# Twenty matmuls on a constant tile, and a later place for the second token half, ahead of and in the first SwiGLU of an encoder trunk

## The chip, the cores and the metric

The kernel runs on one core of a Trainium2 chip. The metric is device time in microseconds of one execution. TensorE does the matrix products (PE in the profile; PEld is its loading of weights), VectorE (DVE) and ScalarE (ACT) the elementwise work, GpSimd (POOL) a little of the setup, SyncE (SP) issues the transfers. Each engine takes its own instructions in the order in which they are queued, and waits where an instruction needs something that isn't there yet.

## What is computed

Two groups of tokens (512 and 256, width 1024) go through two layers with shared weights. Each layer is half a SwiGLU, a mixer, half a SwiGLU, each with an RMSNorm ahead and a residual; a last RMSNorm follows.

```
def swiglu(h, wg, wu, wd):
    return (jax.nn.silu(h @ wg) * (h @ wu)) @ wd

def even_layer(x, f1_n, f1_g, f1_u, f1_d, mix_n, ...):
    x = x + 0.5 * swiglu(rmsnorm(x, f1_n), f1_g, f1_u, f1_d)
...
```

The change concerns the first of the four SwiGLUs: `wg` and `wu` are 1024 x 2816, `wd` is 2816 x 1024, all float32.

## The kernel before

All activations lie transposed: `x[m]`, m = 0 to 7, is a tile of 128 features by 768 tokens. The tokens are treated as two halves of 384 (`HALVES`, h = 0 and 1). Products are made of float32 operands split in a rounded high part and a remainder: `mm3` issues three matmuls (high by high, high by low, low by high). For a weight, the high part is a cast on ACT (`whi`, line 111) and the remainder a subtraction on DVE (`wlo`, line 112); five buffers of each exist.

The gate and up products of the SwiGLU are done by a Strassen-like scheme with seven products in place of eight: the features are cut in m < 4 and m >= 4, the tokens in the two halves, the output columns in pairs of 128-wide tiles ("pairs", `NPAIR` = 11). The right-hand operands are called b11, b21 (first token half, m < 4 and m >= 4), t2, t3, t1, n4, b22 (combinations that need the second half). The left-hand ones are weights or sums of weights (`sums`, line 580). One product for gate or up is 4 x 3 = 12 matmuls with 384 moving columns, so a step for gate and up is 24.

The combinations are prepared from x by `feed` (line 312). For h = 0, `gain_split` makes b11 or b21 directly. For h = 1 and m < 4 it subtracts the first half on DVE (line 327); for m >= 4 it scales by the norm's gain on ACT (line 329); when both features of an index are there, `combine` (DVE, line 348) and `split` (ACT line 193, DVE line 194) make t2. `rest` (line 350) then makes t3, t1, n4 and b22. The norm itself is applied later: `norm_add` squares x on ACT (lines 213, 216) and adds the squares on DVE (line 217); `norm_tok` sums over the features on PE against a tile of ones and takes the inverse root by 13 small DVE steps (lines 258 to 269); `norm_spread` puts the result on a diagonal (lines 247, 249) and spreads it on PE by `onesr`; line 388 copies it to where `hidden` (lines 481 to 484) multiplies by it.

The order on PE is the order in which the program issues; the other engines are ordered by a scheduler at build time. Work that runs beside the products is written as generators, which `tick` advances behind each `mm3` by a clock of the planner, `self.t`: a matmul of n columns adds n/2400 us, at least 0.107, and a float32 one four times that. `norm_half` waits on that clock `DELAY0` = (7, 11) us for the first half and `DELAY1` = (26, 12) for the second ahead of the sums and ahead of the spread. `run_until` sets the clock forward where the program needs a result that isn't issued yet.

The first three pairs (`EARLY`) begin ahead of the rest, in steps that `ORDER` = (0, 1, 0, 1, 0, 2, 1, 2, 2) gives: pair 0's products on b11, pair 1's on b11, pair 0's on b21, pair 1's on b21, pair 0's `hidden(0, 0)`, and so on. A product on b11 is copied from its bank on ACT (tile p, line 497), because b21's products are added into the same bank while the other products need p1 alone. These copies are collected in `copied`: the first two are those of pair 0 (gate, up), the next two those of pair 1. Behind these steps, pair 0 is done in the order p6 (t2), p7 (t3), p5 (t1), p3 (b22), p4 (n4), with `hidden(1, 1)` behind p5, the first that needs the second half's norm.

For the first SwiGLU, the work on the second token half is issued by `second` (line 371). `issue_after(ins)` keeps the instructions of its block that run on the same engine as `ins` (here ACT) behind `ins` in that engine's queue; instructions of the block on other engines get no such bound. In the kernel before, both passes of the loop (first `feed`, then `norm_add`) wait until two copies have been issued by the program, and are queued behind `copied[1]`.

Of the kernel before, what the change touches and what calls it, by code (L numbers as in the profile page):

```python
# [16 lines left out]
P = 128  # L17
# [21 lines left out]
NMASK = 8 * (24 + 32 + 24) + 4 * (40 + 40)  # L39
NE = 30  # L40
EARLY = 3
ORDER = (0, 1, 0, 1, 0, 2, 1, 2, 2)

WTOTAL = 12 * D * FF + 8 * EARLY * P * D + D * 1792 + 2 * D * D + D * 3072 + D * 512
GAP0 = 4.6
# [4 lines left out]
class Trunk:  # L50
# [320 lines left out]
    def second(self):  # L371

        for n in (1, 2):
            while len(self.copied) < 2:
                yield 0.2
            with self.tc.issue_after(self.copied[1]):
                for m in [i // 2 + (0 if i % 2 else 4) for i in range(KD)]:
                    if n == 1:
                        self.feed(m, 1)
                    else:  # L380
                        self.norm_add(m, H, T)
        self.half_done(1)
# [8 lines left out]
    def ffn(self, pre):  # L391
# [42 lines left out]
        def pair(p):  # L434

            early = p < EARLY
            names = ("gate", "up")
# [117 lines left out]
        stages = [pair(p) for p in range(NPAIR)]  # L555
        for p in ORDER:
            next(stages[p])
# [826 lines left out]
    def build(self):  # L1384
        nc = self.nc
        self.ident = self.cp.tile([P, P], F32, tag="ident", name="ident")
        make_identity(nc, self.ident)
        self.ones = self.cp.tile([P, P], F32, tag="ones", name="ones")
        nc.gpsimd.memset(self.ones, 1.0)
        self.onesr = self.cp.tile([P, P], F32R, tag="onesr", name="onesr")  # L1390
        nc.vector.tensor_copy(self.onesr, self.ones)
        self.gains = self.cp.tile([P, KD * len(NORMS)], F32, tag="gains", name="gains")
        nc.scalar.dma_start(self.gains, self.aps["gains"])
        self.ngains = self.cp.tile([P, KD * len(NORMS)], F32, tag="ngains", name="ngains")
        nc.gpsimd.tensor_scalar(out=self.ngains, in0=self.gains, scalar1=-1.0, scalar2=None, op0=ALU.mult)
        self.x = [self.xp.tile([P, T], F32, tag=f"x{m}", name=f"x{m}") for m in range(KD)]
        todo = [KIND[p] for p in self.phases] + [("last", 6)]
        kind = todo[0][0]
        if kind == "f":
            self.ffn_open("right")  # L1400
            self.ffn_tiles()
            self.fw = self.open("work", "left")
        elif kind != "last":
            self.mixer_tiles("right")
        self.norm_begin(todo[0])
        for h, (c0, c1) in enumerate(HALVES):
            for m in range(KD):
                nc.sync.dma_start(self.x[m][:, c0:c1], self.aps["x"][m, :, c0:c1])
                if not (h and kind == "f"):
                    self.final(m, c0, c1)  # L1410
                if h == 0 and m % 4 == 3 and kind == "f":
                    pre = f"{self.phases[0][:2]}_ffn{self.phases[0][3]}"
                    self.first += [self.raw(f"{pre}_w_{n}", 0, KD, m // 4 * 2 * P, P) for n in ("gate", "up")]
            if h and kind == "f":
                self.spawn(self.second())
            elif kind in ("f", "last"):
                self.half_done(h)
            if kind == "last":
                self.drain()
        for i, ph in enumerate(self.phases):  # L1420
            self.following = todo[i + 1]
            if i == 0 and "l1m" in self.phases:
                self.bias_tables()
            if ph == "l1m":
                while self.spare:
                    self.spare.pop(0)()
            if ph == "l0m":
                self.mixer0()
            elif ph == "l1m":
                self.mixer1()  # L1430
            else:
                self.ffn(f"{ph[:2]}_ffn{ph[3]}")
        self.drain()
        for n in list(self.guards)[::-1]:
            self.close(n)
# [103 lines left out]
```

## Time and profile before

| | |
|---|---|
| device time, median of 3 runs | 2689.56 us (2686.41 to 2692.57) |
| profiled execution, span from first to last instruction | 2689.7 us |
| PE busy | 2594.1 us (96%) |
| DVE busy | 2309.7 us (86%) |
| ACT busy | 1399.3 us (52%) |
| first product of the first SwiGLU | at 8.42 us |
| mean granted TensorE clock | 0.981 |

The page gives no time of the profiled execution but its span, so that span stands for it; it is 0.1 us above the median of the runs. In rows of a timeline the columns are start, duration, engine, line, operation, output<-inputs, shapes, and in brackets the idle time ahead with what ended it. Busy rows overlap a little, since an instruction may start before the one ahead of it has drained: what an instruction costs in a full queue is the distance between starts.

### The profile page before, as it was taken

Reading aid. Unit: us, or ns where it says so; the run is one execution under the profiler, and the core shown is the slowest. Engines: PE = TensorE matmul, PEld = TensorE weight load, DVE = VectorE, ACT = ScalarE, POOL = GpSimd, SP = SyncE. Lnnn points to the kernel's source line nnn. Section 1 sums busy time; section 2 is a strip of 40 time slices with the busy share of each in tenths; the row PEclk is TensorE's granted clock in tenths of the full one; section 3 lists DMA queues with packets and bytes.
Section 4 is the critical chain, followed back from the end, with each engine's and each line's share of the span. In section 5 each row is a group of like instructions: output and inputs, shape, how many; then the busy total and the mean of one; then the engine's idle time right before and its main releaser. Section 6 shows DMA issues by size and latency. Waiting matters only on the chain.

```text
span 2689.7 us, 41021 instructions
## 1 busy us (share of the span) xinstructions
PE 2594.1 (96%) x14950; PEld 2530.4 (94%) x14950; DVE 2309.7 (86%) x4865; ACT 1399.3 (52%) x2915; POOL 91.0 (3%) x172
## 2 busy tenths in 40 slices
PE   7999999999999999999999999999999989999997
PEld 6999999977889999999999999988888989999997
DVE  8988888789769988898998888877777699888886
ACT  6545444555655544455654454455555465454443
POOL 0000000000100000000000000012121100000000
PEclk9999999999999999999999999989999999999999
DMA  5332222321222222222322222231211322222121
GB/s 168 111 94 89 79 63 88 132 71 44 79 75 95 73 69 79 66 76 79 95 79 73 69 76 70 83 116 50 62 60 37 95 87 86 79 63 79 63 87 55
DMA packets 82745, 214.78 MB, mean 80 GB/s; under 512 B 19952, under 2 KB 32752, under 8 KB 82544
## 3 DMA queue, kind: packets, MB, share of 16 engines
q1 hardware_dynamic: 82400, 212.14, 24.7%
q8 instruction: 117, 1.92, 0.3%
q14 instruction: 84, 0.69, 0.1%
q10 hardware_dynamic: 144, 0.03, 0.0%
HBM read 202.70 MB, written 15.07 MB: 81 GB/s over the span
## 4 chain that ended last, share of the span: by engine, by line
PE 88%; DVE 8%; ACT 2%; issue 1%; DMA 0%; SPq 0%; DVEq 0%; ACTq 0%
PE ps_mm L137 56%; PE ps_aux L137 31%; DVE wlo L112 1%; PE ps_aux L141 1%; DVE kl L1140 1%; DVE xl L710 1%; ACT whi L111 0%; DMA raw<-in_w 0%; DVE tl L194 0%; DVE qk L1327 0%; DVE kl L1142 0%; ACT xh L709 0%; DVE p L893 0%; DVE p L878 0%; DVE x L677 0%
## 5 line engine op out<-in xcount | busy, mean ns | idle before, releaser
L111 ACT CAST whi<-s 128x512 fp32r<-128x512 f32 x496 | 302.1, 620 | 378.0 <-DVE s L580 142.7
L111 ACT CAST whi<-raw 128x512 fp32r<-128x512 f32 x512 | 309.9, 619 | 260.9 <-PE ps_mm L137 127.2
L112 DVE TENSOR_TENSOR wlo<-s,whi 128x512 fp32r<-128x512 f32 x496 | 335.5, 685 | 74.7 <-ACT whi L111 74.3
L112 DVE TENSOR_TENSOR wlo<-raw,whi 128x512 fp32r<-128x512 f32 x494 | 336.9, 690 | 23.5 <-ACT whi L111 20.4
L137 PE MATMUL ps_aux<-dt,whi 128*128 128x384 f32 x864 | 221.6, 338 | 0.0
L137 PE MATMUL ps_mm<-db,whi 128*128 128x384 f32 x864 | 221.6, 338 | 0.0
L137 PEld LDWEIGHTS ps_mm<-db,whi 128*128 128x128 f32 x864 | 156.8, 188 | 0.0
L137 PEld LDWEIGHTS ps_aux<-dt,whi 128*128 128x128 f32 x864 | 156.8, 188 | 0.0
L137 PE MATMUL ps_mm<-xh,whi 128*128 128x512 f32 (+1 forms) x416 | 148.3, 357 | 2.9 <-ACT xh L709 2.9
L137 PE MATMUL ps_mm<-xl,whi 128*128 128x512 f32 (+1 forms) x416 | 145.0, 348 | 1.1 <-DVE xl L710 1.1
L137 PE MATMUL ps_mm<-db,wlo 128*128 128x384 f32 x432 | 146.0, 338 | 0.0
L137 PE MATMUL ps_aux<-dt,wlo 128*128 128x384 f32 x432 | 145.9, 338 | 0.0
L137 PE MATMUL ps_mm<-xh,wlo 128*128 128x512 f32 (+1 forms) x416 | 144.5, 347 | 0.0
L580 DVE TENSOR_TENSOR s<-raw,raw 128x512 f32<-128x512 f32 x124 | 83.4, 685 | 21.6 <-DMA raw<-in_w 21.4
L467 ACT COPY u<-ps_mm 128x384 f32<-128x384 f32 x176 | 83.6, 475 | 35.0 <-PE ps_mm L137 34.9
L472 DVE TENSOR_TENSOR u<-ps_aux,u 128x384 f32<-128x384 f32 x176 | 97.1, 551 | 5.0 <-PE ps_aux L137 3.8
L137 PE MATMUL ps_aux<-dh,whi 128*128 128x384 f32 x384 | 98.5, 338 | 0.7 <-DVE x L677 0.7
L884 ACT ACTIVATE p<-p,st 128x192 f32<-128x192 f32 (+2 forms) x144 | 68.8, 480 | 54.9 <-DVE st L882 54.9
L632 DVE TENSOR_TENSOR x<-ps_aux,x 128x384 f32<-128x384 f32 x160 | 86.6, 552 | 11.2 <-PE ps_aux L137 11.0
L580 DVE TENSOR_TENSOR s<-raw 128x512 f32<-128x512 f32 x124 | 84.9, 685 | 11.8 <-DMA raw<-in_w 11.3
L137 PE MATMUL ps_mm<-oh,whi 128*128 128x384 f32 x256 | 89.4, 349 | 4.0 <-DVE x L861 4.0
L632 DVE TENSOR_TENSOR x<-ps_mm,x 128x384 f32<-128x384 f32 x160 | 87.0, 551 | 6.0 <-PE ps_mm L137 5.9
(438 smaller groups left out, 8204.5 us busy)
## 6 DMA issues: line engine op xcount, KB each, us to landing
raw<-in_w SPq DMA_DIRECT2D x342, 512.0 KB, 3.6
xdm<-x SPq DMA_DIRECT2D x16, 384.0 KB, 2.4
x<-in_x SPq DMA_DIRECT2D x16, 192.0 KB, 5.7
x<-xdm SPq DMA_DIRECT2D x8, 384.0 KB, 3.8
xold<-xdm SPq DMA_DIRECT2D x8, 384.0 KB, 3.2
out_y<-y SPq DMA_DIRECT2D x8, 384.0 KB, 2.5
tab<-skew SPq DMA_DIRECT2D x8, 256.0 KB, 4.5
raw<-in_w SPq DMA_DIRECT2D x8, 256.0 KB, 2.6
```

Source lines behind the costliest of these rows:

```text
L111: nc.scalar.copy(hi, src)
L112: (eng or nc.gpsimd).tensor_tensor(out=lo, in0=src, in1=hi.bitcast(F32), op=ALU.subtract)
L137: self.nc.tensor.matmul(out, lhsT=lhsT, rhs=rhs, start=start, stop=stop, **kw)
L141: self.nc.tensor.transpose(out, src, self.ident)
L467: nc.scalar.copy(e[n, out], bank[key, n])
L472: nc.vector.tensor_tensor(out=t, in0=bank[key, n], in1=t, op=ALU.add)
L580: f = lambda o, x, y, op: self.nc.vector.tensor_tensor(out=o, in0=x, in1=y, op=op)
L632: nc.vector.tensor_tensor(out=o, in0=ps, in1=o, op=ALU.add)
L710: nc.vector.scalar_tensor_tensor(out=lo, in0=src, scalar=gain, in1=hi.bitcast(F32), op0=ALU.mult, op1=ALU.subtract)
L884: nc.scalar.activation(outs[i], outs[i], AF.Exp, bias=nm[:, i : i + 1], accum_out=sm[:, i : i + 1])
L1140: nc.vector.tensor_tensor(out=kl[a, c0:c1], in0=s, in1=kh[a, c0:c1].bitcast(F32), op=ALU.subtract)
```

## The change

Ahead of the loop that loads x, 20 matmuls are issued on `onesr`, a 128 x 128 tile of ones in the rounded format, into a tile of the psum pool `aux` that nobody reads. They do not go through `mmul`, so the planner's clock does not see them.

In `second`, both passes now wait until four copies have been issued by the program. The first pass (`feed`) is queued on ACT behind `copied[3]`, the copy of pair 1's up product; the second pass (`norm_add`) stays behind `copied[1]`.

```
+WARM = 20
...
         for n in (1, 2):
-            while len(self.copied) < 2:
+            while len(self.copied) < 4:
                 yield 0.2
-            with self.tc.issue_after(self.copied[1]):
+            with self.tc.issue_after(self.copied[3 if n == 1 else 1]):
                 for m in [i // 2 + (0 if i % 2 else 4) for i in range(KD)]:
                     if n == 1:
                         self.feed(m, 1)
                     else:
                         self.norm_add(m, H, T)
...
         self.norm_begin(todo[0])
+        if kind == "f":
+            warm = self.psum(self.aux, "aux")
+            for _ in range(WARM):
+                nc.tensor.matmul(warm[:, :P], lhsT=self.onesr, rhs=self.onesr, start=True, stop=True)
         for h, (c0, c1) in enumerate(HALVES):
```

More of the change, by code (lines that the diff above doesn't have):

```diff
@@ L41 @@
 EARLY = 3
+WARM = 20
 ORDER = (0, 1, 0, 1, 0, 2, 1, 2, 2)
@@ L373, in second @@
         for n in (1, 2):
-            while len(self.copied) < 2:
+            while len(self.copied) < 4:
                 yield 0.2
-            with self.tc.issue_after(self.copied[1]):
+            with self.tc.issue_after(self.copied[3 if n == 1 else 1]):
                 for m in [i // 2 + (0 if i % 2 else 4) for i in range(KD)]:
@@ L1405, in build @@
         self.norm_begin(todo[0])
+        if kind == "f":
+            warm = self.psum(self.aux, "aux")
+            for _ in range(WARM):
+                nc.tensor.matmul(warm[:, :P], lhsT=self.onesr, rhs=self.onesr, start=True, stop=True)
         for h, (c0, c1) in enumerate(HALVES):
```

## The prediction

> **What bounds the kernel now.** I read the page's first part, then the busy time by stretch, the waits, and the timelines of PE, ACT and DVE for the first 115 us, which is all that the change can touch directly.
>
> ```profile
> span 2689.7 us, 41021 instructions
> ...
> PE 2594.1 (96%) x14950; PEld 2530.4 (94%) x14950; DVE 2309.7 (86%) x4865; ACT 1399.3 (52%) x2915; POOL 91.0 (3%) x172
> ```
>
> PE is busy for 96% of the span, so what can be won is PE's idle and slow time. The busy times by stretch (length, then PE, PEld, DVE, ACT, POOL, clock, DMA share, GB/s) put the first SwiGLU beside a later one. The first and third row run from the first product to the first product on b22, the second and fourth from there to the first product on t2 of pair 2; the fifth is a PE-bound stretch of the first SwiGLU's middle.
>
> ```profile
> 8.42:65.85 57.43, 46.38 (x232) 44.18 (x233) 53.88 (x131) 42.05 (x89) 0.00 (x0) 0.91 0.47 150
> 65.85:114.45 48.60, 46.21 (x265) 45.57 (x264) 47.14 (x89) 26.12 (x54) 0.00 (x0) 1.00 0.34 110
> 788.87:833.47 44.60, 40.45 (x228) 40.12 (x227) 43.26 (x108) 32.88 (x68) 0.00 (x0) 0.96 0.34 99
> 833.47:881.18 47.71, 46.22 (x265) 45.89 (x264) 47.42 (x90) 26.37 (x54) 0.00 (x0) 1.00 0.26 85
> 150.00:200.00 50.00, 50.00 (x289) 50.00 (x288) 43.70 (x80) 22.85 (x45) 0.00 (x0) 1.00 0.33 93
> ```
>
> The reading that decides: in the first 106 us PE has gaps, but DVE hardly has any. DVE idles 57.43 - 53.88 = 3.55 us before the first b22 product and 48.60 - 47.14 = 1.46 us behind it, 5.0 us in all. The second SwiGLU shows how close to full DVE gets at its best here: 44.60 - 43.26 = 1.34 and 47.71 - 47.42 = 0.29 us idle. From 150 us on PE is full and DVE has 6.3 us in 50 free, so there what PE has won is kept to the end.
>
> The longest wait of PE in the first 120 us, behind the one for the first weights (total, times, longest):
>
> ```profile
> PE ps_mm L137 <- ACT p L497: 6.0, 1, 6.0
> ```
>
> The change touches this wait. ACT's timeline shows its cause:
>
> ```profile
> 14.99 0.47 ACT L497 COPY p<-ps_mm 128x384 f32<-128x384 f32 x1
> 15.35 2.70 ACT L111 CAST whi<-raw 128x512 fp32r<-128x512 f32 x5
> 17.95 0.62 ACT L329 ACTIVATE tmp<-x,gains 128x384 f32<-128x384 f32 x1
> ...
> 18.89 1.34 ACT L216 ACTIVATE sq<-x 128x384 f32<-128x384 f32 x3
> ...
> 29.36 0.46 ACT L497 COPY p<-ps_mm 128x384 f32<-128x384 f32 x1
> ```
>
> The copy at 14.99 is copied[1], that at 29.36 copied[2]. The copies of pair 1's first products (copied[2], and copied[3] behind it) stand behind the combining of the second token half in ACT's queue, which begins at 17.95. PE may not add b21 of pair 1 to those banks before they are copied:
>
> ```profile
> 8.42 0.69 PE L137 MATMUL ps_mm<-b110h,whi 128*128 128x384 f32 x1 [8.42 <-ACT whi L111]
> ...
> 10.59 0.52 PE L137 MATMUL ps_mm<-b112h,whi 128*128 128x384 f32 x1
> 10.91 0.52 PE L137 MATMUL ps_mm<-b112l,whi 128*128 128x384 f32 x1
> ...
> 13.42 0.34 PE L137 MATMUL ps_mm<-b111h,wlo 128*128 128x384 f32 x1
> 13.59 0.34 PE L137 MATMUL ps_mm<-b112h,whi 128*128 128x384 f32 x1
> ...
> 29.87 0.69 PE L137 MATMUL ps_mm<-b210h,whi 128*128 128x384 f32 x1 [6.02 <-ACT p L497]
> ...
> 38.48 0.45 PE L137 MATMUL ps_mm<-b110h,whi 128*128 128x384 f32 x1 [2.39 <-DVE sg L481]
> ```
>
> PE was done with pair 0's b21 products at 29.87 - 6.02 = 23.85. Starts are 0.32 us apart early on and 0.17 later: the array runs at half speed at first. Two more such stretches follow the two gaps:
>
> ```profile
> 29.87:33.16 3.29, 3.29 (x10) 3.29 (x11) 3.29 (x9) 3.16 (x9) 0.00 (x0) 0.52 0.11 17
> 40.07:43.27 3.20, 3.20 (x11) 3.20 (x11) 2.76 (x6) 1.30 (x3) 0.00 (x0) 0.50 0.36 48
> ```
>
> with a granted clock of 0.52 and 0.50. Ten matmuls at 0.32 instead of 0.17 cost 1.5 us each time.
>
> **Part 1, the 20 matmuls on onesr.** The trace has no warm-up; the nearest rows are matmuls of the same shape, and the cast that makes onesr:
>
> ```profile
> 1.11 0.23 DVE L1391 CAST onesr<-ones 128x128 fp32r<-128x128 f32 x1 [1.11 <-POOL ones L1389]
> 660.00 0.27 PE L137 MATMUL ps_aux<-swh,vhl 128*128 128x128 f32 x1
> 660.11 0.28 PE L137 MATMUL ps_aux<-swh,vhh 128*128 128x128 f32 x1
> ```
>
> One costs 0.11 us at full speed and, scaled by 0.32/0.17, 0.21 at half. Twenty from 1.34 on take 2.2 to 4.2 us and end between 3.5 and 5.6; even at 0.32 each they end at 7.7, ahead of 8.42. PE is empty there, so they cost nothing, and the tile of aux that they use is not wanted before the first norm's sums, behind the first 48 products. The gain: if the clock were full at 8.42, the twelve matmuls up to about 12.5 would take 0.15 less each, 1.8 us. But PE then idles for 2.8 us or more ahead of the first product, and the trace shows the 2.39 us gap before 38.48 followed by 1.6 us at full and then 3.2 us at half speed. The Trainium skill (TensorE: Matmul & The Clock Gate, "Why this matters for your kernels") says that gaps up to about 3 us between bursts do no harm; by it the whole 1.8 us come. The row at 40.07 speaks against it. Bounds -1.8 to 0; I take -0.4, nearer the row, and because DVE is the limit soon after.
>
> **Part 2, the order on ACT.** Behind copied[3] now stand ACT's scalings of m = 4 to 7 and, through DVE, the splits of t2, t3, t1, n4, b22. The squares of the second half keep copied[1] as their bound, so they fill ACT first: eight at 1.34/3 = 0.45, 3.6 us. The five casts end near 18, and pair 1's first products at about 23.85 - 24 x 0.17 - 0.7 (the sums of the first norm) = 19, so the two copies come between 19 and about 23, and PE starts pair 1's b21 at 23.85 or little later. The 6.02 us of idle go, and the 1.5 us at half speed behind it.
>
> What is late next is DVE. Combining that began on ACT at 17.95 begins at 20 to 24. If DVE had nothing else, it would idle for the difference, up to 6 us; but the additions into acc, the subtractions of m = 0 to 3, the first norm's small steps and the weight remainders need none of this. Bounds 0 to 6; I take 0.5, near the end that DVE's full row supports. All of DVE's work up to b22 remains. PE, no longer waiting for the copy, waits instead for hidden(0, 0) and for the sums and remainders of t2's weights. So the gain is not 7.5 us but what DVE's idle can shrink: to the second SwiGLU's values, (3.55 - 1.34) + (1.46 - 0.29) = 3.4 us. I take -3.4.
>
> **Part 3, what moves with it.** second() ends, and starts the second half's norm, only when four copies exist. On the planner's clock (0.16 per matmul of 384) that is 9.4 instead of 4.3, since 24 matmuls and the first norm's sums (1.28) come first. The sums of the second norm, due 26 behind the planner's next look, move from 30.8 to 35.9, and PE's order with them: from the third matmul of t3 to the twelfth of t1, 33 matmuls later. The spread stays where hidden(1, 1) asks for it, right behind t1. The rows of both norms that bound the chain between sums and spread, the busy one and the one at the kernel's end with nothing in between:
>
> ```profile
> 55.11 0.72 PE L137 MATMUL ps_aux<-ones,acc 128*128 128x1 f32 x6
> ...
> 65.15 0.87 PE L137 MATMUL ps_aux<-diag,onesr 128*128 128x384 f32 x2 [1.40 <-DVE diag L249]
> ...
> 2676.00 0.83 PE L137 MATMUL ps_aux<-ones,acc 128*128 128x1 f32 x6 [1.86 <-DVE acc L217]
> 2680.26 1.17 PE L137 MATMUL ps_aux<-diag,onesr 128*128 128x384 f32 x2 [3.42 <-DVE diag L249]
> ```
>
> The chain takes 65.15 - 55.83 = 9.3 us there, 3.4 here. Only 12 matmuls, 2.1 us, will cover it, so the gap of 1.40 becomes 1.3 to 7.2. Most of what DVE does in the gap is owed anyway; of the extra 0 to 5.8 I take 0.5.
>
> **Sum.** -0.4 - 3.4 + 0.5 + 0.5 = -2.8 us. Against the profiled span of 2689.7 (0.1 above the median of the three runs, 2689.56) that is 2686.9. About 0.2%, 5.4 us, is what a measurement of this kernel can tell from no change.
>
> **Rivals.** Faster: PE keeps its whole gain. That needs 4 to 5 us of DVE's work to slip behind 114 us, where DVE has 6.3 in 50 free. For it: n4's operands and the hidden products are not needed before b22. Against it: DVE is 97% busy from 65.85 to 114.45 too. Then 6.0 + 1.5 + 0.4 go: 2681.8, and 2680.4 with the full warm start.
>
> Slower: the second norm's chain takes the place of the wait removed. If the sums come 12 matmuls ahead of the spread and DVE still threads a weight piece between every two small steps, PE idles 7.2 us behind t1 (+5.8) and then runs ten matmuls at half speed (+1.5), while DVE, short of free weight buffers, gains nothing by it; with 1 us saved by the other parts that is 2689.7 + 7.3 - 1 = 2696. It decides from a chain of about 7.3 us on (2.1 cover + 1.4 old gap + 0.4 + 3.4 gained elsewhere). For it: 9.3 us in this very place. Against it: 3.4 us when nothing is threaded in.
>
> No effect: ACT's order puts the copies behind weight casts that wait for PE (with five buffers, the eleventh cast needs pair 0's b21 products to be over, at 23.85), and the same work merely changes places: 2689.5.
>
> **How the numbers follow.** The forecast, 2686.9, has a chance of 0.48, its own range 2683.5 to 2690 (the full warm start and another 2 us of DVE's idle gone; 3 us of new idle, half the bound). The faster rival has 0.26, the slower one 0.18, no effect 0.08. Faster by over 0.2% (under 2684.2): the faster rival and 0.08 of the forecast, 0.34. Slower by over 0.2% (over 2695.0): 0.12 of the slower rival. Within: 0.54. The range reaches from 2679.5, past the faster rival's bound, to 2695.0.
>
> **What would show it.** Right: twenty small matmuls from about 1.4 us, then PE idle up to 8.4; copies of p at 19 to 24; no wait of 6 us on ACT p; DVE busy above 96% up to the first b22 product, which starts at 62 to 64; sums of the second norm after 12 matmuls of t1, and a gap behind t1 longer than 1.4. Wrong: DVE idle over 5 us before b22 (slower rival), b22 before 60 us (faster rival), the copies still near 29 (no effect), or differences behind 120 us, where nothing should change.

## The result: slower by 0.5%

The changed kernel takes 2704.07 us (median; 2699.17 to 2706.22) against 2689.56 (2686.41 to 2692.57) for the kernel before: ratio 1.0049, 95% interval 1.0037 to 1.0061. The forecast was 2686.9, the range ended at 2695.0.

First the page of the kernel after: the span, and busy time with share of the span.

```profile
span 2700.2 us, 41071 instructions
...
PE 2602.3 (96%) x14970; PEld 2536.5 (94%) x14970; DVE 2310.8 (86%) x4865; ACT 1398.8 (52%) x2915; POOL 90.7 (3%) x172
```

This execution took 2702.02 us of device time, 1.8 more than its span; the prediction had set the span of before equal to its time. The spans differ by 10.5 us, the medians by 14.5. (The added constant shifts the line numbers by one.)

Where the 10.5 us arise is read from two products that both kernels have in the same place of PE's order: the first on t3 of pair 2, and the first on b11's operand (db) in the third down step (pairs 3 and 4). From PE's timeline of before, then of after:

```profile
117.02 0.34 PE L137 MATMUL ps_mm<-t30h,whi 128*128 128x384 f32 x1
...
255.43 0.51 PE L137 MATMUL ps_mm<-db,whi 128*128 128x384 f32 x2
```

```profile
1.39 4.53 PE L1410 MATMUL ps_aux<-onesr 128*128 128x128 f32 x20 [1.39 <-DVE onesr L1392]
8.95 0.69 PE L138 MATMUL ps_mm<-b110h,whi 128*128 128x384 f32 x1 [3.04 <-ACT whi L112]
...
34.32 0.69 PE L138 MATMUL ps_aux<-diag,onesr 128*128 128x384 f32 x1 [4.16 <-DVE diag L250]
36.14 0.69 PE L138 MATMUL ps_aux<-diag,onesr 128*128 128x384 f32 x1 [1.14 <-ACT diag L248]
39.80 0.69 PE L138 MATMUL ps_mm<-b110h,whi 128*128 128x384 f32 x1 [2.98 <-DVE sg L482]
...
61.19 0.72 PE L138 MATMUL ps_aux<-ones,acc 128*128 128x1 f32 x6
...
68.62 1.12 PE L138 MATMUL ps_aux<-diag,onesr 128*128 128x384 f32 x2 [4.52 <-DVE diag L250]
...
121.53 0.34 PE L138 MATMUL ps_mm<-t30h,whi 128*128 128x384 f32 x1
...
259.21 0.62 PE L138 MATMUL ps_aux<-dt,whi 128*128 128x384 f32 x2 [2.76 <-ACT whi L112]
260.44 0.44 PE L138 MATMUL ps_aux<-dt,wlo 128*128 128x384 f32 x1 [0.61 <-DVE wlo L113]
...
265.41 0.51 PE L138 MATMUL ps_mm<-db,whi 128*128 128x384 f32 x2
```

PE is 121.53 - 117.02 = 4.5 us late in pair 2 and 265.41 - 255.43 = 10.0 in the third down step; it stays there to the end. So there are two losses, 4.5 and 5.5 us. (0.5 of the 4.5 is there from the start: the first product comes at 8.95 and not 8.42. Over the kernels run here it comes between 8.39 and 9.99, and at 10.84 in e8.) Three things are to be read in these rows:

- The 6.02 us wait on ACT p is gone; in its place stand 4.16, 1.14 and 2.98 us on diag, diag and sg, 8.3 in all against 6.02 + 2.39 = 8.4 before.
- Behind t1, PE waits 4.52 us for the second norm's diagonal, where it was 1.40.
- At 259 us there is a gap of 2.76 + 0.61 us that before doesn't have at all.

The busy times by stretch of after (length, PE, PEld, DVE, ACT, POOL, clock, DMA share, GB/s): from the first product to the first on b22, from there to pair 2, and the three half-speed stretches behind the gaps.

```profile
8.95:69.53 60.58, 46.22 (x232) 42.71 (x233) 54.51 (x131) 42.06 (x89) 0.00 (x0) 0.89 0.47 144
69.53:118.96 49.43, 47.93 (x265) 47.61 (x265) 47.50 (x89) 26.45 (x54) 0.00 (x0) 0.96 0.34 105
68.62:73.69 5.07, 5.07 (x15) 4.93 (x16) 2.77 (x6) 1.99 (x5) 0.00 (x0) 0.50 0.70 244
39.80:42.85 3.05, 3.05 (x10) 3.05 (x10) 3.05 (x7) 0.60 (x2) 0.00 (x0) 0.50 0.32 40
261.64:264.84 3.20, 3.20 (x11) 3.20 (x11) 2.75 (x6) 0.08 (x1) 0.00 (x0) 0.50 0.71 193
```

DVE's idle time was to shrink; it grew, from 3.55 to 60.58 - 54.51 = 6.07 us ahead of b22 and from 1.46 to 1.93 behind it.

On ACT the change does what it says. The copies of pair 1's products come ten us earlier, and the combining starts behind them:

```profile
19.14 0.47 ACT L498 COPY p<-ps_mm 128x384 f32<-128x384 f32 x1
...
20.81 0.48 ACT L498 COPY p<-ps_mm 128x384 f32<-128x384 f32 x1
21.19 0.62 ACT L330 ACTIVATE tmp<-x,gains 128x384 f32<-128x384 f32 x1
```

### The profile page after: what moved, and what is told of

It reads as the page before. It is cut to its first block, busy times and chain, and to the rows that moved or that the text cites. A ratio compares the mean times of both kernels' runs of the same rounds, so it can differ in the third digit from the quotient of the medians.

```text
span 2700.2 us, 41071 instructions
## 1 busy us (share of the span) xinstructions
PE 2602.3 (96%) x14970; PEld 2536.5 (94%) x14970; DVE 2310.8 (86%) x4865; ACT 1398.8 (52%) x2915; POOL 90.7 (3%) x172
## 3 DMA queue, kind: packets, MB, share of 16 engines
q8 instruction: 118, 1.93, 0.3%
## 4 chain that ended last, share of the span: by engine, by line
PE 88%; DVE 8%; ACT 2%; issue 1%; DMA 1%; SPq 0%; DVEq 0%; ACTq 0%
PE ps_mm L138 56%; PE ps_aux L138 31%; DVE wlo L113 1%; PE ps_aux L142 1%; DVE kl L1141 1%; DVE xl L711 1%; DVE tl L195 0%; DMA raw<-in_w 0%; ACT whi L112 0%; DVE qk L1328 0%; DVE kl L1143 0%; ACT xh L710 0%; DVE p L894 0%; DVE p L879 0%; DMA x<-in_x 0%
```

## The experiments

Theory: the second norm's later place in PE's order makes both losses, the new order of the second token half wins nothing because another wait of the same length stands behind the one removed, and the 20 matmuls do nothing. Rivals: that the matmuls or the ACT order cost time themselves, and that DVE's amount of work explains everything.

### e1: the 20 matmuls alone

```
 before, and only:
+            for _ in range(20):
+                nc.tensor.matmul(warm[:, :P], lhsT=self.onesr, rhs=self.onesr, ...)
```

> The kernel before plus the 20 matmuls alone; second() is as before. Theory A (the moved second norm and the other order on DVE cost the time): this kernel has no gap above 1.6 us behind t1 and none near 259 us; the first t2 product of pair 2 behind the 1.50 us gap (114.45 before, 118.96 with the whole change) comes at 114 to 116, the time is 2689 to 2692. Theory B (the 20 matmuls cost it, through an ACT queue in which the copies stand ahead of the gain casts): that landmark comes at 118 or later and the time is 2699 or more. For the clock: the first ten products still run 0.32 us apart, since PE idles 3 us between the 20 matmuls and the first product.

2689.26 us (2687.63 to 2695.49) against 2689.67; ratio 0.9998 (0.9990 to 1.0007). The first product came at 8.55, behind 2.63 us of idle PE, and starts were 0.32 apart until 13.61, fifteen products in place of the ten expected. No effect is seen: the interval reaches from 2.7 us won to 1.9 lost. In this one trace the first product on t3 of pair 2 comes at 118.64, 1.6 us behind before's.

### e8: 44 matmuls, up to the first product

```
-WARM = 20
+WARM = 44      (otherwise as e1)
```

> e1 with 44 matmuls on the tile of ones instead of 20: they end at about 1.4 + 4.5 + 24 x 0.11 = 8.6 us, so PE has no gap of 3 us ahead of the first product. If the gap is why the first products ran at half speed, they now start 0.17 us apart from the first on, the 48 products on b11 take 8.3 to 9.5 us instead of 10.5 to 12.3. If DVE bounds the stretch, the landmark behind pair 1 still stays within 1.5 us of 114.45 and the time at 2687 to 2691.

2691.0 us (2688.75 to 2695.58); ratio 1.0005 (0.9996 to 1.0014). PE's timeline of e8, and one row of its busy times by stretch:

```profile
1.39 9.65 PE L1410 MATMUL ps_aux<-onesr 128*128 128x128 f32 x44 [1.39 <-DVE onesr L1392]
10.84 0.63 PE L138 MATMUL ps_mm<-b110h,whi 128*128 128x384 f32 x1
...
15.11 0.48 PE L138 MATMUL ps_mm<-b110l,whi 128*128 128x384 f32 x1
15.43 0.34 PE L138 MATMUL ps_mm<-b110h,wlo 128*128 128x384 f32 x1
```

```profile
10.90:15.43 4.53, 4.53 (x16) 4.53 (x15) 4.53 (x10) 4.37 (x11) 0.00 (x0) 1.00 1.04 388
```

There is no gap ahead of the first product, which is pushed back to 10.84. The array still runs at half speed, 9.65/44 = 0.22 us for each small matmul (0.11 at 660 us of before) and 0.32 for the products, up to 15.43: 14 us of unbroken work. The gap behind 20 matmuls is therefore not what kept the array slow, or not alone; more matmuls don't help either. The clock column says 1.00 here, against the distances between the starts.

### e2: the new order of the second token half alone

```
 after, and only:
-WARM = 20
+WARM = 0
```

> The change to second() alone, no matmuls ahead. Theory A: the gap behind t1 is 4 to 5 us and is followed by about 3 to 5 us at half speed, the landmark comes at 117 to 119, the 2.8 us gap near 259 is there too, since DVE is queued in the same order there as with the whole change; time 2698 to 2703. Theory B: landmark at 114 to 116, time within 3 us of the kernel before.

2701.14 us (2700.36 to 2703.0); ratio 1.0045 (1.0031 to 1.0058). The trace has after's gaps: 5.30 + 0.88 + 2.04 us on diag, diag and sg, 4.51 behind t1, 2.75 at 258.73. The loss is the second part's of the change.

### e3 and e4: the second norm's sums back in their old place

```
 after (e3), after without the 20 matmuls (e4), and:
-        yield from self.norm_half(h, *(DELAY1 if h else DELAY0))
+        d0, d1 = DELAY1 if h else DELAY0
+        yield from self.norm_half(h, d0 - 5.12 if h and self.nxt[1] == 0 else d0, d1)
```

> The whole change, but the sums of the second norm keep their old place in PE's order (DELAY1's 26 is 5.12 less for this norm alone, so they stand behind the third matmul of t3 again). Theory A: the gap behind t1 falls from 4.5 to 2 us or less and no half speed follows; the landmark comes at 113 to 116. DVE's queue has the two sums of the third down step three places earlier than with the whole change, so the gap at 259 is half as long or gone; time 2688 to 2696. If the place of the second norm doesn't matter (the combining behind copied[3] is late by itself), the gap behind t1 and the landmark stay at 4.5 us and 118 to 119, time 2700 or more.

> As the run before, but without the 20 matmuls: the change to second() with the second norm's sums in their old place. Theory A: as the run before within 2 us, landmark 113 to 115, time 2686 to 2695, the copies of pair 1 ahead of the combining and no wait on ACT's copy. If the late combining itself costs, the landmark is at 117 or later. If DVE bounds this stretch, as predicted, PE's saved 6 us reappear as waits on DVE's diagonal and on sg, and the landmark is within 2 us of 114.45.

e3: 2690.45 us (2688.79 to 2694.41), ratio 1.0005 (0.9996 to 1.0014). e4: 2689.69 us (2686.91 to 2692.21), ratio 1.0001 (0.9992 to 1.0009). Everything that was lost is back, and nothing is won that can be told from the spread (e4's interval: 2.2 us won to 2.4 lost). In e4's trace the gap behind t1 is 0.6 us, that of the third down step 0.65, but PE waits as long as ever ahead of pair 2's b11. On t3 of pair 2 PE is level with before in e4 (116.81 against 117.02) and 2.3 us late in e3 (119.35), where the first product was 0.85 late already; that is a little more than expected. PE's timeline of e4:

```profile
33.71 0.69 PE L138 MATMUL ps_aux<-diag,onesr 128*128 128x384 f32 x1 [5.30 <-DVE diag L250]
35.28 0.69 PE L138 MATMUL ps_aux<-diag,onesr 128*128 128x384 f32 x1 [0.88 <-ACT diag L248]
38.01 0.69 PE L138 MATMUL ps_mm<-b110h,whi 128*128 128x384 f32 x1 [2.04 <-DVE sg L483]
```

And DVE's from the first small step of the first norm to the diagonals, in e4:

```profile
20.01 0.16 DVE L259 TENSOR_SCALAR sm<-ps_aux 128x3 f32<-128x3 f32 x1 [0.61 <-PE ps_aux L138]
...
32.98 0.68 DVE L250 TENSOR_SCALAR diag<-ident,yh 128x128 fp32r<-128x128 f32 x3
```

The chain takes 13 us, because a piece of combining, an addition into acc or a weight remainder stands between nearly every two steps. It did so before the change too, 11 us long, hidden by the wait for p, which ended at 29.87. DVE's timeline of before, and ACT's with the second diagonal:

```profile
19.62 0.16 DVE L258 TENSOR_SCALAR sm<-ps_aux 128x3 f32<-128x3 f32 x1 [0.51 <-PE ps_aux L137]
...
30.77 0.67 DVE L249 TENSOR_SCALAR diag<-ident,yh 128x128 fp32r<-128x128 f32 x3
```

```profile
32.49 0.99 ACT L247 ACTIVATE diag<-ident,yl 128x128 fp32r<-128x128 f32 x3
```

DVE's idle time, which was to shrink, stayed: from e4's first product to its first on b22 it is 56.04 - 52.55 = 3.49 us, against 3.55 before.

```profile
8.94:64.98 56.04, 46.20 (x232) 42.83 (x233) 52.55 (x129) 41.28 (x88) 0.00 (x0) 0.91 0.44 135
```

### e5: the second norm's later place alone

```
 before, and only:
+        d0, d1 = DELAY1 if h else DELAY0
+        yield from self.norm_half(h, d0 + 5.12 if h and self.nxt[1] == 0 else d0, d1)
```

> The kernel before with one number changed: DELAY1's 26 is 5.12 more for the second norm of the first SwiGLU, so that its sums stand 33 matmuls later in PE's order, where the whole change puts them; second() and the start of PE are as before. Theory A (this move alone is the loss): gap of 4 to 5 us behind t1 and several us at half speed behind it, DVE queued near 259 us as with the whole change and a 2.8 us gap there, time 2697 to 2702. If the loss needs the later combining too: landmark within 2 us of 114.45, time 2688 to 2693.

2700.53 us (2695.82 to 2702.67); ratio 1.0036 (1.0023 to 1.0048). PE's timeline of e5:

```profile
30.51 0.69 PE L137 MATMUL ps_mm<-b210h,whi 128*128 128x384 f32 x1 [6.02 <-ACT p L498]
...
66.01 1.11 PE L137 MATMUL ps_aux<-diag,onesr 128*128 128x384 f32 x2 [3.09 <-DVE diag L249]
...
258.90 0.61 PE L137 MATMUL ps_aux<-dt,whi 128*128 128x384 f32 x2 [2.76 <-ACT whi L111]
```

With the wait for p untouched, the later place of the sums alone brings the longer gap behind t1 (3.09 us, short of the 4 to 5 expected) and also the gap at 259 us, and most of the loss.

### e9: the order at the third down step alone

What joins a norm at 60 us to a gap at 259? DVE's queue. The scheduler orders it at build time, and after's order differs from before's up to the third down step. The two sums of pair 4's weights, from which its first cast is made, stand ahead of pair 5's sg and v before, behind them after. DVE's timeline of before, then of after:

```profile
247.70 0.68 DVE L580 TENSOR_TENSOR s<-raw,raw 128x512 f32<-128x512 f32 x1
...
249.84 0.55 DVE L481 TENSOR_TENSOR sg<-ps_mm,acc 128x384 f32<-128x384 f32 x1
```

```profile
255.97 0.56 DVE L484 TENSOR_TENSOR v<-ps_mm,acc 128x384 f32<-128x384 f32 x1 [1.56 <-PE ps_mm L138]
...
257.77 0.68 DVE L581 TENSOR_TENSOR s<-raw,raw 128x512 f32<-128x512 f32 x1
```

v waits for the last product of pair 5, so behind it the sum comes 10.1 us later, and PE, 4.5 late by itself, gets the weight late by 2.8. The weights themselves were there: in after the last load issued ahead of the sums landed at 251.1.

```
 after, and for the third down step of the first SwiGLU:
+    a, s, s2 = self.down_begin(pre, range(3, 5))     # loads and sums, ahead of hidden(1, 0) of pair 5
+    with self.tc.issue_after(self.sum_ins):          # the later sum of pair 4
         hidden(1, 0, bank["Y", "gate"], bank["Y", "up"])
```

> The changed kernel, and of the third down step in the first SwiGLU (pairs 3 and 4) the two sums of pair 4's weights (s<-raw,raw and s<-s,raw) are kept ahead of sg and v of pair 5 in the order of DVE, as they stand in the kernel before; no other order on DVE, ACT, SP or PE moves except within a few places of there. Theory (the second loss, 5.5 us between 117 and 255 us, is nothing but the place of these two sums in the queue of DVE): the gap of 2.75 us before 259.21, the 0.61 behind it and the half speed from 261.64 on go; everything up to 117 us stays, 4.5 us late, with the 4.51 us gap behind t1; time 2704.07 - 5.5 = 2698.5, 2696.5 to 2700.5. Rival (the gap comes from what arrives late there, the weights or a backlog of DVE, and the order only follows it): a gap of over 2 us stays near 259, 2702 to 2705.

2694.91 us (2690.85 to 2699.56); ratio 1.0021 (1.0012 to 1.0030). The gap at 259 us is gone:

```profile
260.30 0.44 PE L140 MATMUL ps_aux<-dt,wlo 128*128 128x384 f32 x1 [0.38 <-DVE wlo L115]
```

and the 4.5 us behind t1 are still there. The mechanism is shown. In e9's trace the way from the first product on t3 of pair 2 to the first on db takes 139.8 us, against 143.9 in after and 138.4 before: 4.1 of the 5.5 us are back at this place. The medians give more, 1.0049 - 1.0021 = 0.0028, 7.5 us; the intervals reach 3.2 and 2.4 us to either side, so neither 5.5 nor 4.1 is excluded.

### e10 and e11: less work on DVE, with and without the wait for p

```
 in rest(), first SwiGLU only:
+    for n in ("t3", "t1", "n4", "b22"):
+        self.b[n] = [(hi, hi) for hi, lo in self.b[n]]     # and no remainder is computed
 e10: before; e11: e4. In both, the sums of the third down step as in e9
```

The high part is then multiplied a second time in the remainder's place; PE's matmuls are the same in number and shape.

> The kernel before, in which the first SwiGLU's 16 remainders of t3, t1, n4 and b22 are left out (the rounded high part is read in their place, so that part of the result is only of the precision of its high part; PE does as many matmuls); 16 DVE operations of 0.47 to 0.55 us, some 8 us, are gone before 66 us. The sums of the third down step are held ahead of sg and v as in the kernel before. Theory (DVE limits the first 115 us, so the wait for p was idle time that DVE's work would have forced anyway): time falls, but the wait of PE on ACT p of about 6 us stays: 2681 to 2686. Rival (PE's own chain limits, and DVE only looks full): less than 2 us, 2687.5 to 2690.

> The same 16 remainders left out of the kernel that has the change's new order of the second token half and the second norm's sums at their old place (no matmuls on the constant tile). Theory (with DVE relieved, the wait for p that the change takes away is at last worth something): 2 to 6 us less than the kernel before with the same remainders left out, 2677 to 2683, with no wait on ACT p and waits on diag and sg shorter than the 8.2 us they take with the remainders in. Rival (the small steps of the first norm and ACT, not the amount of work on DVE, set those waits): the two lean kernels within 1.5 us of each other, and the waits on diag and sg still 7 to 8 us.

e10: 2685.43 us (2681.57 to 2686.83), ratio 0.9981 (0.9972 to 0.9990). e11: 2685.8 us (2682.93 to 2689.0), ratio 0.9986 (0.9977 to 0.9995). Sixteen DVE operations less are worth over 4 us to either, so DVE's load does cost time here. But the kernel without the wait for p is no faster than the one with it (6.01 us in e10), and the theory for e11 fell. PE's timeline of e11:

```profile
34.29 0.69 PE L140 MATMUL ps_aux<-diag,onesr 128*128 128x384 f32 x1 [5.36 <-DVE diag L253]
35.86 0.69 PE L140 MATMUL ps_aux<-diag,onesr 128*128 128x384 f32 x1 [0.88 <-ACT diag L251]
37.71 0.69 PE L140 MATMUL ps_mm<-b110h,whi 128*128 128x384 f32 x1 [1.16 <-DVE sg L491]
```

7.4 us in all, against 6.01 + 1.41 = 7.4 in e10. In e11 the first norm's chain still takes 13 us (20.54 to 33.56), as in e4, since none of the 16 remainders stood between its steps. So the waits follow the chain, and these two kernels don't show what less work between its steps would do. What the fewer operations win, they win behind the chain: in e10 pair 2's b11 comes at 38.55 (38.48 before), but the first product on b22 at 60.48 (65.85 before). There DVE's amount of work does count.

### e6: part of DVE's work on GpSimd

```
 e4, and:
-            nc.vector.tensor_tensor(out=self.acc[:, a:b], in0=self.acc[:, a:b], in1=sq, op=ALU.add)
+            eng = nc.gpsimd if a and self.nxt[1] == 0 else nc.vector
+            eng.tensor_tensor(out=self.acc[:, a:b], in0=self.acc[:, a:b], in1=sq, op=ALU.add)
```

> e4 (second() changed, second norm in its old place, no matmuls ahead), with the additions of the second half's squares into acc on GpSimd instead of DVE: seven times 0.47 us less for DVE. If DVE's amount of work bounds the stretch up to b22, the first b22 product comes 2 to 4 us earlier than in e4 (64.98). If the first norm's chain and its place in the queue bound it, and not DVE's amount, b22 moves by less than 1 us. DVE's queue at the third down step has the sums as late as with the whole change, so a gap of about 2.8 us near 255 us and 3 us at half speed are expected there, about 4 us; time 2687 to 2694.

2707.02 us (2702.08 to 2709.14); ratio 1.0062 (1.0049 to 1.0075). The wait on diag grew to 6.95 us and that on sg to 4.04. GpSimd's timeline of e6, and the rows of the small steps there in the view of the tile sm (ns: shortest, median, longest):

```profile
26.86 7.56 POOL L219 TENSOR_TENSOR acc<-acc,sq 128x384 f32<-128x384 f32 x5 [4.15 <-ACT sq L217]
```

```profile
L269 DVE TENSOR_TENSOR sm<-sm x3: 157/959/980, 21.7 to 28.7; 128x3 f32<-128x3 f32 x3
...
L271 DVE SCALAR_TENSOR_TENSOR sm<-sm x3: 151/952/997, 23.7 to 32.1; 128x3 f32<-128x3 f32 x3
```

The same steps take at most 0.156 us in e4. While GpSimd adds, a step of the chain takes up to six times as long: fewer operations on DVE, and a longer chain. Neither expectation fits: the first product on b22 comes 1.5 us later than in e4, at 66.45. Of the whole loss 10 us are there on t3 of pair 2 (126.88 against e4's 116.81), with another wait of 4.49 us for a weight at 122.51, and 4.5 us arise by the third down step, where the gap of 2.76 us stands again, as expected.

### e7 and e12: the chain made short

```
 e7: e4, and the combining waits for the first norm and is queued on DVE behind its diagonals;
     second norm's delay 15.4 us shorter than before (e4: 5.12)
 e12: e4, with a delay 16.5 us shorter than before, and
      the diagonals are made right behind the first norm's sums:
+            diags = self.diagonals(y) if h == 0 and self.nxt[1] == 0 else None
      second(), t2's combining:   + issue_after(self.diag)
      second(), squares; rest():  + issue_after(self.vop)    # v of hidden(0, 0)
      hidden(0, 0) with high priority; sums of the third down step as in e9
```

> e4, but the second half's combining is queued behind the first norm's diagonal on DVE too (and, in the program, behind the first spread), so that nothing of it is threaded between the 13 small steps; the second norm's sums keep their old place. If the threading is what holds the first spread back, the spread comes at 27 to 30 instead of 33.7 and the first product of pair 2 at 30 to 33 instead of 38.0. If DVE's amount bounds the stretch all the same, PE then waits longer ahead of t2, the first b22 product stays at 63 to 67 and the time within 3 us of e4 (2689.7); if not, b22 comes 3 to 6 us earlier and the time is 2684 to 2687.

> The changed kernel without its 20 matmuls, with the second norm's sums earlier (sixth t2 weight, 55 products ahead of the spread), the third down step's sums held where the kernel before has them, and three moves of program order in the first SwiGLU: the first norm's diagonals are made right behind its sums instead of 11 us of the planner later; the combining of the second token half (t2) is queued on DVE behind them; and the second half's squares, t3, t1, n4 and b22 are queued behind the first two multiplications of hidden(0, 0) (sg, v). Nothing is left out. Theory (what took the place of the wait for p is the first norm's chain, 12 us from the sums to the diagonals because other work stands between its small steps, and then sg behind still more of that work; run bare the chain takes 2.7 us): diagonals at 22 to 23, PE goes through b21 of pairs 0 and 1 to about 29 without a stop, and the waits on p, diag and sg ahead of pair 2's b11 shrink from 8.2 to under 4 us; 4 to 5 us won by then, of which 3 or more stay: 2684.5 to 2687.5. Rival (DVE's amount of work limits the stretch up to 115 us, whatever its order): the waits on diag and sg shrink too, but new ones of the same sum appear ahead of t2, t3 or t1, on their operands or weights; 2688.5 to 2691.

e7: 2699.37 us (2696.54 to 2701.82), ratio 1.0034 (1.0021 to 1.0047). e12: 2696.01 us (2694.31 to 2702.95), ratio 1.0028 (1.0017 to 1.0040). In both the chain runs bare; in e12 its first step starts at 20.41 and the diagonals at 23.07, 2.7 us later. PE's timeline of e7, then of e12:

```profile
29.73 0.44 PE L138 MATMUL ps_mm<-b110h,whi 128*128 128x384 f32 x1 [1.53 <-DVE sg L483]
39.65 0.69 PE L138 MATMUL ps_mm<-b210h,whi 128*128 128x384 f32 x1 [5.49 <-ACT p L499]
```

```profile
33.08 0.69 PE L141 MATMUL ps_mm<-b110h,whi 128*128 128x384 f32 x1 [3.92 <-DVE sg L500]
48.56 0.45 PE L141 MATMUL ps_mm<-t20h,whi 128*128 128x384 f32 x1 [2.79 <-ACT whi L115]
...
69.34 0.69 PE L141 MATMUL ps_aux<-b220h,wlo 128*128 128x384 f32 x1 [3.44 <-DVE wlo L116]
```

The waits on diag are gone and PE reaches pair 2's b11 5.4 us ahead of before (38.48) in e12, 8.7 in e7. All of it is given back: in e7 at the next copy of p, which stands behind the combining on ACT; in e12 ahead of t2 and b22, whose weights wait for sums and remainders that DVE now does later, and in half-speed stretches behind those gaps (51.74 to 56.69 and 69.34 to 73.66). e7's first product on b22 (64.19) lies where DVE's amount of work was to put it, its time above either expectation. The theory for e12 fell with its number. Its rival, DVE's amount of work, isn't shown by it either: DVE idled more than in e4, 30.00 - 24.58 = 5.4 us between 45 and 75 against 2.1. Whether some order of DVE would keep the 5 us stays open; none that was run and computes everything is faster than the kernel before.

## Why the prediction was wrong, step by step

Three terms of the sum failed. The order on ACT won nothing (-3.4 forecast), the second norm's later place cost some 5 us (0.5 forecast), and 5.5 us arose behind 120 us (nothing forecast). The first alone would have left the time inside the range; the other two took it out.

**Part 1, the matmuls: the number held, by luck.** -0.4 was forecast, e1 measured -0.4 with an interval of over 2 us either way that holds zero. The place (1.39, idle PE to 8.95) was right. The reason was not: the prediction put the half speed at the first products down to the gap between, and e8 has the half speed without a gap.

**Part 2, the order on ACT: the step that failed is the price, "what DVE's idle can shrink", -3.4.** The copies came at 19.14 and 20.81, inside the forecast's 19 to 23, and the 6.02 us went. The waits in their place are on DVE, as "what is late next is DVE" has it. But the gain was sized by DVE's idle time, as if DVE's work were one sum, and that idle time didn't shrink (3.49 us in e4). What was late next was one chain on DVE, the first norm's small steps, which ended at nearly the same time as the wait removed: in after 8.3 us for 8.4. The prediction wrote "PE waits instead for hidden(0, 0)" and didn't price it, though the rows of that chain were in the trace of before. e4 (1.0001, at most 2.2 us won) and e11 (no better than e10) show the term as about 0. That the chain took the place of the wait is shown; why nothing is won with a short chain either (e7, e12) stays open.

**Part 3, the second norm: the right place and the wrong value.** The sums came after exactly 12 matmuls of t1, at 61.19, and the gap was inside the bounds of 1.3 to 7.2. DVE's timeline of after shows the chain:

```profile
61.95 0.16 DVE L259 TENSOR_SCALAR sm<-ps_aux 128x3 f32<-128x3 f32 x1 [0.59 <-PE ps_aux L138]
...
66.63 0.16 DVE L269 TENSOR_TENSOR sm<-sm 128x3 f32<-128x3 f32 x1
...
67.89 0.67 DVE L250 TENSOR_SCALAR diag<-ident,yh 128x128 fp32r<-128x128 f32 x3
```

Threaded up to 66.63, then bare, as DVE had nothing else left. From the sums' end to the spread it is 68.62 - 61.91 = 6.7 us, between the rows of 9.3 and 3.4. The term "I take 0.5" was the one mis-sized: the extra gap is 4.52 - 1.40 = 3.1 us, and the half speed of the spread and of thirteen products behind it adds 2.1 (68.62 to 73.69), together 5.2. "Most of what DVE does in the gap is owed anyway" was no reason: it keeps DVE busy, but PE is the one that is late. The loss of 4.5 us by pair 2 is this term less the small differences around it; in e4, without it, PE is level with before there.

**The slower rival** had the right mechanism and price (+5.8 and +1.5 at most), and even the tell-tale, DVE idle over 5 us before b22 (6.07). Its condition was a chain of about 7.3 us, 3.4 of it for what is gained elsewhere; the chain took 6.7, and as those 3.4 didn't come, it decided all the same. e9, with only this loss left, takes 2694.9 against the rival's 2696; the 2704 of the whole change holds the other loss too. Its 0.18 was too low: the one row against it, 3.4 us, came from a place where DVE has nothing else to do.

**"Differences behind 120 us, where nothing should change": wrong by 5.5 us.** The changed code ends there, but the scheduler's order of DVE does not. e9 shows it: with two sums put back in DVE's queue the gap at 259 us goes. No rival had this, and the range ended too low for it.

**The base** was sound by accident: a run's time is its span and 1.8 us, so the profiled execution took some 2691.5 us, not 2689.7, but the median of the runs is 2689.56.

## What to carry to other kernels

Before a wait is priced as a gain, look for the chain that ends next at the same consumer: walk back from the consumer's other operands in the old trace, and take the distance between the two ends as the most that can be gained, not the length of the wait. Here the second diagonal was ready at 32.49 + 0.99 = 33.48 in the old trace and PE read it from 35.59 on: 2.1 us, not 6.02. A reduction that is moved later in a queue needs its whole chain's length as cover, at the length it has among the other work in that place; and when a scheduler orders the queues, compare the order of all engines to the end of the program, since a moved instruction can swap two others far behind it.

## What the runs showed of the hardware

**No warm-up was seen at the start.** e8's 14 us of unbroken matmuls up to 15.43 stayed at half speed by the distances between starts, while half-speed stretches later end after 3.2 us (261.64 to 264.84 in after). The Trainium skill (TensorE: Matmul & The Clock Gate, "Why this matters for your kernels") advises a warm-up of at least 4 us of matmuls for accurate benchmarks; here the measurement differs. Full speed, 0.17 us between starts, begins 3.1 to 6.3 us behind the first product in the nine traces without small matmuls and 3.4 to 6.3 us behind it in the five with them. Whether matmuls on the tile of ones don't count, or the start of an execution is slow for another reason, no run separates. Busy transfers aren't the reason: in after PE runs at full speed from 12.38 to 14.97 with the DMA engines as busy as ahead of it (share 1.05 in both).

**GpSimd holds up small VectorE steps.** Up to 1.0 us instead of 0.16 in e6. The Trainium skill (SBUF — State Buffer, "Who interferes with whom") says that a VectorE instruction with two inputs in SBUF contends with a GpSimd instruction that reads SBUF, and calls the ports that they share an exclusive lock. The long rows shown agree with that. A cast with one input (yh<-sm) took 0.96 us too, which that sentence doesn't cover.

**The spread of one kernel's runs goes with its clock.** Of the 15 runs of the kernel before beside e5, the three with a mean granted clock of 0.985 took 2685.6 to 2687.8 us, the seven with 0.981 2691.1 to 2693.1. The stretches at half speed behind 300 us, where the order of PE's instructions is the same, counted from the distances between the starts (four matmuls or more), add up to some 60 us in the profiled runs of before and after, and to 45 to 50 in e9's and e12's. A single trace can thus be several us off the median: e12's span is 2.8 us above before's, its median 6.6.
